# A two-layer encoder with a hierarchical mixture of experts: the first four experts as one block of four, two weight tiles outside the ring, fewer double buffers

## Chip, cores, metric

One core of a Trainium2 chip runs the whole program in one launch. The metric is the device time of a launch in microseconds (us); the time before is the median of three runs.

## What is computed

A sequence of 256 tokens of width 1024, in float32, goes through two layers. Each layer has an attention mixer (layer 0: differential and latent attention side by side; layer 1: dilated attention), a layer norm, a mixture of experts, and another layer norm. The mixture is where most bytes are: 32 experts per layer, each with a gate and an up matrix of 1024 x 512 and a down matrix of 512 x 1024. Every token is sent to two experts of one group:

```
coarse = xf @ w_group + b_group;  g_sel = argmax(coarse)
fine = (xf @ w_route + b_route)[group g_sel]
top_v, top_i = top_k(fine, 2)
gate = softmax(coarse)[g_sel] * softmax(top_v)
eid = g_sel * 8 + top_i
hb = silu(xb @ w_gate[e]) * (xb @ w_up[e]);  y = hb @ w_down[e]
out[token] += gate * y
```

The reference pads each expert to blocks of 256 rows; the result does not depend on that.

## The kernel before, in words

**Weights.** All large weights pass through `ring`, 18 buffers of 128 x 2048 float32 (one "piece" of 1,048,576 bytes each), issued on the queue of SP in program order. One expert is six pieces: two halves each of gate, up and down. A piece can be issued when the buffer that it takes, 18 allocations back, has been read for the last time. One more piece per layer, `lead`, has a tile of its own in the pool of the expert stage, outside the ring.

**Blocks.** The experts of a layer are worked off in blocks, listed in `BLOCKS` as (experts in the block, index of the first). A block fills the 128 stationary columns of TensorE: either two experts with 64 token slots each, or four experts with 32 slots each (`CAP`, `SMALL`). Experts 0 to 3 (`FIXED`) stand in the first two blocks, two experts with 64 slots each. The other 28 are sorted on the device by how many tokens they got (`ordered`); the four fullest (`HEAVY`) make two more blocks of two, and the other 24 make six blocks of four. Ten blocks in all. The numbers of the sorted experts, `ids`, are read by SP from a tile before it can issue their weights (`value_load`, L587); the weights of experts 0 to 3 need no such number, so they can be fetched while the router has not run.

**What one block does** (`expert_block`): the gate products `g` (L606), the up products `u` (L606), a small stage that makes `wcol` and `selT` for putting results back (`slot_side`), the nonlinearity and a transpose to `hT` (`hidden`), the down products `y` (L627), and `combine`, which adds the block's results to the residual `r` with matmuls `cb` (L563). The inputs of a block's experts are collected by matmuls with a 0/1 matrix `sel` into `xg` (`gather`, L532), for two blocks at a time. For the first pair only the 128 columns of block 0 are collected ahead; `fetch` collects the columns of block 1 in two parts inside block 0, one before `y` and one behind it.

**Fetching ahead.** Near the end of the mixer, `load_block` issues the 12 pieces of block 0; at the start of the expert stage it issues 6 pieces of block 1, and then `lead`, the last down piece of block 1 (`LATE`). Together with `lead` that is 19 pieces before the first product of the stage gives a buffer back. 5 more pieces of the 24 of experts 0 to 3 follow, and then the pieces of the sorted experts.

**Too many tokens.** When an expert has more tokens than its slots, `extra_block` runs behind the last block but one, once for each further 64 tokens (`lite` says by how much a slot count is below 64). It loads the whole expert again through POOL's queue, in pieces of 128 x 1024.

Of the kernel before, what the change touches and what calls it, by code (L numbers as in the profile page):

```python
# [28 lines left out]
SORTED = EXPERTS - FIXED  # L29
BLOCKS = [(2, i) for i in range(0, FIXED + HEAVY, 2)]  # L30
BLOCKS += [(4, i) for i in range(FIXED + HEAVY, EXPERTS, 4)]
MAX_EXTRA = (2 * T) // (SMALL + 1)
ALPHA = (2 * 2) ** 0.25
# [10 lines left out]
CLOCK = 43  # L44
LATE = 1, 11
WO_ORDER = (0, 4, 1, 5, 2, 6, 3, 7), tuple(range(8))
# [14 lines left out]
def trunk(ctx, tc, xT_d, x_d, wab_d, wla_d, wuq_d, wukv_d, woab_d, wc_d, wocd, wr_d, rb_d, gate_d, up_d, down_d,  # L61
# [324 lines left out]
    def route(pool, lg_ps, mvs, layer):  # L386
# [75 lines left out]
        def ordered(W):  # L462
# [22 lines left out]
            lite = t([32], "lite")  # L485
            v.memset(lite[:, 0:FIXED], 0.0)
            v.tensor_scalar(lite[:, FIXED:], place, float(HEAVY), float(CAP - SMALL), op0=OP.is_gt, op1=OP.mult)
# [21 lines left out]
    def slot_side(pool, sel, ws, ne, cap, name):  # L509
        n = ne * cap  # L510
        b = bank("slot" + name)
        for c in range(2):
            nc.tensor.matmul(b[0:n, 0:ne], lhsT=sel[:, c], rhs=ws[:, c], start=c == 0, stop=c == 1)
        for c in range(2):
            nc.tensor.transpose(b[0:n, 128 * (c + 1):128 * (c + 2)], sel[:, c], ident)  # L515
        wcol = pool.tile([128, 1], F32, tag="wcol", name="wcol" + name)
        for s in range(ne):
            nc.vector.tensor_copy(wcol[cap * s:cap * s + cap], b[cap * s:cap * s + cap, s:s + 1])  # L518
        selT = pool.tile([128, 256], F32R, tag="selT", name="selT" + name)
        nc.scalar.activation(selT[0:n], b[0:n, 128:384], AF.Copy)  # L520
        return wcol, selT, b

    def gather(xg, x, which, sel, o, n, name, evict=lambda kk: 1, first=False, todo=range(KK)):
        per = 512 // n
        for k0 in range(todo[0], todo[-1] + 1, 8 if first else per):
            bs = [bank("xg" + name) for _ in range(2 if first else 1)]
# [69 lines left out]

    def expert_block(pool, layer, p, ws, xg, side, r, fetch, rows):
        name = f"_{layer}_{p}"
        ne = BLOCKS[p][0]
        cap = 128 // ne  # L600
        o = 128 * (p % 2)
        gu = [bank("g" + name), bank("u" + name)]
# [19 lines left out]
        for k2 in range(2):  # L622
            for h in range(2):
                for k in (2 * k2, 2 * k2 + 1):
                    for s in range(ne):
                        w0 = k % 2 * 1024 + h * 512
                        nc.tensor.matmul(y_ps[h][cap * s:cap * s + cap], lhsT=hT[:, k, cap * s:cap * s + cap],  # L627
                                         rhs=ws[2, s, k // 2][:, w0:w0 + 512], start=k == 0, stop=k == 3)
        if p == 0:
            fetch(range(4, KK))  # L630
        return combine(pool, y_ps, side, 128, r, name, p == 0, accs), accs

    def extra_block(pool, layer, x, key, W, extra, lite, r):
# [10 lines left out]
        ohb = oh[:, None, :].to_broadcast([128, 2, 32])  # L644
        pr = pool.tile([128, 2, 2, 32], F32, tag="x_pr", name="x_pr")
# [4 lines left out]
        rem = pool.tile([128, 32], F32, tag="x_rem", name="x_rem")  # L650
        v.tensor_tensor(rem, extra, oh, op=OP.mult)
# [34 lines left out]
    def moe(layer, acc, x_in, xn, after):  # L686
        with tc.tile_pool(name=f"moe{layer}", bufs=2) as pool:
            lead = pool.tile([128, PIECE], F32, name=f"lead{layer}", bufs=1)
            xs = keep.tile([128, 2, D], F32, tag="xT", name=f"xs{layer}")
            ws = moe_w[layer]  # L690

            load_block(ws, layer, 0)
            load_block(ws, layer, 1, RING - 12)
            block, i = LATE
            e = BLOCKS[block][1] + i % 2
            nc.sync.dma_start(lead, down_d[layer][e, :, PIECE:2 * PIECE])
            ws[block][2, i % 2, 1] = lead
            lg_ps, mvs, last_lg, clk = mixer_norm(pool, acc, x_in, xn, layer)
# [4 lines left out]
            W = ids = None  # L703
            for q in range(len(BLOCKS) // 2):
                name = f"_{layer}_q{q}"
                ne, first = BLOCKS[2 * q]
                cap = 128 // ne
                if first < FIXED:
                    keys = key[:, :, first:first + 2 * ne]
                else:  # L710
                    keys = keyS[:, :, first - FIXED:first - FIXED + 2 * ne]
                sel = select(pool, keys, 2 * ne, cap, name, 1 if q == 0 else 2)
                xg = keep.tile([128, KK, 4 * CAP], F32, tag=("r", "gb")[q % 2], name="xg" + name)

                gather(xg, xs, 2 * layer, sel, 0, 2 * CAP if q == 0 else 4 * CAP, name,
                       (lambda kk: kk % 2 or kk > 3) if q == 0 else (lambda kk: kk // 2 % 2), q == 0)
# [88 lines left out]
    def heads_ab(pool, xT):  # L805
# [234 lines left out]
    def heads_c(pool, x, ws, res, gb):  # L1040
# [254 lines left out]
```

## Time and profile before

| | |
|---|---|
| time, median of 3 runs | 1176.53 us (1175.67 to 1176.67) |
| the profiled execution's own time | 1176.07 us |
| its span, first to last instruction | 1174.4 us |
| bytes moved | 445.80 MB, mean 380 GB/s over the span |
| TensorE busy | 1000.5 us (85%) |
| mean granted clock of TensorE | 0.956 |

The span is what the views below divide up; 1.67 us of the profiled execution lie outside it. "Busy" of TensorE (PE) counts matmuls whose ends are modelled, so 85% is not 85% of its peak. The views give the rate of all DMA engines in GB/s for any stretch of the span.

### The profile page before, as it was taken

How to read it: one execution, taken by the hardware profiler on the slowest of the kernel's cores; microseconds unless marked ns; L12 is line 12 of the kernel's file. 1: busy time of each engine (PE TensorE's matmuls, PEld its weight loads, DVE VectorE, ACT ScalarE, POOL GpSimd, SP SyncE). 2: the span in 40 equal slices, each digit the busy share in tenths (PEclk: the TensorE clock that was granted, in tenths of full speed). 3: DMA queues.
4: the chain of work that ended last, by engine and by line, in shares of the span. 5: the costliest groups of instructions: out<-in, count | busy, mean ns of one | idle time of the engine just before them, and what ended most of it. 6: DMA issues, size and time to landing. Idle time of an engine off the chain costs nothing. (4 is left out here: it accounts for less than half of the span.)

```text
span 1174.4 us, 14832 instructions
## 1 busy us (share of the span) xinstructions
PE 1000.5 (85%) x5568; PEld 478.2 (41%) x5568; DVE 374.5 (32%) x860; ACT 226.2 (19%) x495; POOL 50.8 (4%) x57
## 2 busy tenths in 40 slices
PE   8999999997787778778889999999977877697775
PEld 7787534342141213112578876343421311131222
DVE  5786822221020101010487768322210101010103
ACT  5565211010010001000445643110100100010001
POOL 0002000000000000000331120000000000000001
PEclk9999999999898989898999999999998989898897
DMA  9966798999999999999995566989999999999994
GB/s 362 424 235 241 286 427 352 427 422 427 427 427 427 426 425 427 427 425 427 426 412 180 156 235 254 427 351 426 424 427 426 426 428 427 425 426 426 425 427 187
DMA packets 65292, 445.80 MB, mean 380 GB/s; under 512 B 7680, under 2 KB 8448, under 8 KB 12992
## 3 DMA queue, kind: packets, MB, share of 16 engines
q1 hardware_dynamic: 62496, 436.15, 89.8%
q0 software_dynamic: 2432, 8.13, 2.0%
q8 instruction: 45, 0.74, 0.2%
q10 hardware_dynamic: 288, 0.52, 0.1%
q14 instruction: 31, 0.25, 0.1%
HBM read 443.73 MB, written 1.05 MB: 379 GB/s over the span
## 5 line engine op out<-in xcount | busy, mean ns | idle before, releaser
L606 PE MATMUL u<-w,xg_q 128*32 128x512 f32 (+1 forms) x1024 | 221.3, 705 | 57.8 <-DMA w<-in_up_dram 57.8
L627 PE MATMUL y<-w,hT 128*32 128x512 f32 (+1 forms) x1008 | 206.9, 602 | 36.4 <-DMA w<-in_down_dram 22.2
L606 PE MATMUL g<-w,xg_q 128*32 128x512 f32 (+1 forms) x1024 | 182.9, 627 | 43.7 <-DMA w<-in_gate_dram 36.3
L606 PEld LDWEIGHTS u<-w,xg_q 128*32 128x32 f32 (+1 forms) x1024 | 52.8, 132 | 210.2 <-DMA w<-in_up_dram 105.6
L627 PEld LDWEIGHTS y<-w,hT 128*32 128x32 f32 (+1 forms) x1008 | 55.6, 116 | 173.9 <-issue 92.6
L542 DVE TENSOR_TENSOR h<-h,u 128x512 f32<-128x512 f32 x20 | 13.8, 688 | 324.2 <-PE u L606 324.2
L606 PEld LDWEIGHTS g<-w,xg_q 128*32 128x32 f32 (+1 forms) x1024 | 46.4, 121 | 166.5 <-issue 91.6
L556 ACT ACTIVATE yh<-y,wcol 128x512 fp32r<-128x512 f32 x40 | 27.5, 687 | 395.0 <-PE y L627 395.0
L557 DVE SCALAR_TENSOR_TENSOR yl<-y,wcol,yh 128x512 fp32r<-128x512 f32 x40 | 29.9, 748 | 221.9 <-ACT yh L556 221.9
L532 PE MATMUL xg_q<-sel_q,xs 128*128 128x256 f32 (+1 forms) x384 | 74.3, 346 | 0.0
L532 PEld LDWEIGHTS xg_q<-sel_q,xs 128*128 128x128 f32 x384 | 63.6, 190 | 9.3 <-issue 1.9
L541 ACT ACTIVATE h<-g 128x512 f32<-128x512 f32 x20 | 11.9, 597 | 224.4 <-PE g L606 224.4
L518 DVE COPY wcol<-slot 32x1 f32<-32x1 f32 (+1 forms) x64 | 9.9, 155 | 140.6 <-PE slot L515 139.7
L572 DVE TENSOR_TENSOR x<-cb,x 128x512 f32<-128x512 f32 x64 | 40.7, 682 | 6.2 <-PE cb L563 5.9
L296 ACT ACTIVATE xg_q<-xg_q,pv 128x256 f32<-128x256 f32 (+1 forms) x60 | 26.9, 512 | 69.0 <-PE xg_q L532 66.0
L247 POOL DMA_DIRECT2D gb<-in_lnrow_dram x8 | 4.3, 542 | 665.7 <-PE u L606 653.8
L520 ACT ACTIVATE selT<-slot 128x256 fp32r<-128x256 f32 x20 | 7.7, 383 | 113.9 <-DVE wcol L518 113.9
L563 PE MATMUL cb<-yl,selT 128*128 128x512 f32 x72 | 26.5, 427 | 0.0
L563 PE MATMUL cb<-yh,selT 128*128 128x512 f32 x72 | 26.1, 421 | 0.0
L297 DVE TENSOR_SCALAR xg_q<-xg_q,pv 128x256 f32<-128x256 f32 (+1 forms) x36 | 17.5, 524 | 20.7 <-PE xg_q L532 19.8
L547 PE MATMUL hT<-con,h 128*128 128x128 f32 x80 | 13.1, 286 | 11.2 <-DVE h L542 10.7
L164 ACT ACTIVATE ec<-ec,stc 128x256 f32<-128x256 f32 x32 | 15.9, 498 | 16.6 <-DVE stc L162 16.6
(1060 smaller groups left out, 1277.9 us busy)
## 6 DMA issues: line engine op xcount, KB each, us to landing
w<-in_gate_dram SPq DMA_DIRECT2D x128, 1024.0 KB, 19.5
w<-in_up_dram SPq DMA_DIRECT2D x128, 1024.0 KB, 19.5
w<-in_down_dram SPq DMA_DIRECT2D x124, 1024.0 KB, 19.4
wqkc<-in_wc_dram SPq DMA_DIRECT2D x8, 1024.0 KB, 19.3
wqk<-in_wab_dram SPq DMA_DIRECT2D x4, 1024.0 KB, 13.3
wo<-in_woab_dram SPq DMA_DIRECT2D x4, 1024.0 KB, 11.3
gb<-in_lnrow_dram POOLq DMA_DIRECT2D x8, 512.0 KB, 8.3
wvc<-in_wc_dram SPq DMA_DIRECT2D x4, 1024.0 KB, 18.2
```

What stands on the lines that cost most here:

```text
L164: marks["exp"] = nc.scalar.activation(e[:, c], t[:, c], AF.Exp, bias=st[:, c:c + 1], scale=scale, accum_out=st[:, 2 + c:3 + c])
L296: return nc.scalar.activation(out, src, AF.Identity, bias=bb, scale=g)
L297: return nc.vector.tensor_scalar(out, src, g, bb, op0=OP.mult, op1=OP.add)
L532: nc.tensor.matmul(out[kk], lhsT=x[:, c, kk * 128:(kk + 1) * 128], rhs=sel[:, c, o:o + n], start=not first and c == 0, stop=c == 1 and (no ...
L542: nc.vector.tensor_tensor(h[0:n], h[0:n], u_ps[0:n], op=OP.mult)
L547: turn = nc.tensor.transpose(bv[:, k, 0:n], h[0:n, k * 128:(k + 1) * 128], ident[0:n, 0:n])
L556: last = nc.scalar.activation(yh[0:n, h], y_ps[h][0:n], AF.Copy, scale=wcol[0:n])
L557: nc.vector.scalar_tensor_tensor(yl[0:n, h], y_ps[h][0:n], wcol[0:n], yh[0:n, h].bitcast(F32), op0=OP.mult, op1=OP.subtract)
L563: last_mm = nc.tensor.matmul(b, lhsT=selT[0:n, c * 128:(c + 1) * 128], rhs=y[0:n, h], start=j == 0 and not accs, stop=j == 1)
L572: nc.vector.tensor_tensor(o, b, o, op=OP.add)
L606: up = nc.tensor.matmul(gu[j][cap * s:cap * s + cap], lhsT=xg[:, kk, o + cap * s:o + cap * s + cap], rhs=ws[j, s, kk // 4][:, kk % 4 * 512 ...
L627: nc.tensor.matmul(y_ps[h][cap * s:cap * s + cap], lhsT=hT[:, k, cap * s:cap * s + cap], rhs=ws[2, s, k // 2][:, w0:w0 + 512], start=k == ...
```

## The change

The first four experts become one block of four, with 32 slots each; nine blocks instead of ten, and `GROUPED` says which blocks share a `gather`: block 0 alone, then (1, 2), (3, 4), (5, 6), (7, 8). `fetch` is gone. Two tiles `leads` hold the second down halves of experts 2 and 3 (`LATE = 22, 23`), and `load_block` in the mixer issues 18 pieces (`RING`) of block 0. `lite` of experts 0 to 3 becomes 32. To make room, `selT`, `hT`, `x_oh` and `x_rem` have one buffer instead of two, and `x_pr` and `x_xg` share the buffers of `fo` and `hT`.

```diff
-BLOCKS = [(2, i) for i in range(0, FIXED + HEAVY, 2)]
+BLOCKS = [(4, 0)] + [(2, i) for i in range(FIXED, FIXED + HEAVY, 2)]
 BLOCKS += [(4, i) for i in range(FIXED + HEAVY, EXPERTS, 4)]
+GROUPED = [(0,)] + [(p, p + 1) for p in range(1, len(BLOCKS), 2)]
-LATE = 1, 11
+LATE = 22, 23
-            v.memset(lite[:, 0:FIXED], 0.0)
+            v.memset(lite[:, 0:FIXED], float(CAP - SMALL))
-        selT = pool.tile([128, 256], F32R, tag="selT", name="selT" + name)
+        selT = pool.tile([128, 256], F32R, tag="selT", name="selT" + name, bufs=1)
-        hT = pool.tile([128, 4, 128], F32, tag="hT", name="hT" + name)
+        hT = pool.tile([128, 4, 128], F32, tag="hT", name="hT" + name, bufs=1)
-            fetch(range(0, 4))
-        if p == 0:
-            fetch(range(4, KK))
-        xg = pool.tile([128, KK, CAP], F32, tag="x_xg", name="x_xg", bufs=1)
+        xg = pool.tile([128, KK, CAP], F32, tag="hT", name="x_xg", bufs=1)
-            lead = pool.tile([128, PIECE], F32, name=f"lead{layer}", bufs=1)
+            leads = [pool.tile([128, PIECE], F32, name=f"lead{layer}{i}", bufs=1) for i in range(2)]
+            for lead, i in zip(leads, LATE):
+                nc.sync.dma_start(lead, down_d[layer][i % 4, :, PIECE:2 * PIECE])
+                ws[0][2, i % 4, 1] = lead
             load_block(ws, layer, 0)
-            load_block(ws, layer, 1, RING - 12)
-            for q in range(len(BLOCKS) // 2):
+            for q, ps in enumerate(GROUPED):
-                ne, first = BLOCKS[2 * q]
-                cap = 128 // ne
+                ne, first = BLOCKS[ps[0]]
+                cap, n = 128 // ne, 128 * len(ps)
-                xg = keep.tile([128, KK, 4 * CAP], F32, tag=("r", "gb")[q % 2], name="xg" + name)
+                xg = keep.tile([128, KK, n], F32, tag=("r", "gb")[q % 2], name="xg" + name)
-        load_block(moe_w[0], 0, 0)
+        load_block(moe_w[0], 0, 0, RING)
```

On SP's queue in layer 0, at the start of the expert stage, before the change (a name `w_0_1_1_0` is layer, block, expert within the block, half; the tensor behind the arrow says whether it is gate, up or down):

```order
L76 DMA w_0_1_0_1_1223<-in_gate_dram 128x2048
L76 DMA w_0_1_1_1_1225<-in_gate_dram 128x2048
L696 DMA lead_1217<-in_down_dram 128x2048
L76 DMA w_0_1_0_0_1227<-in_up_dram 128x2048
L76 DMA w_0_1_1_0_1229<-in_up_dram 128x2048
L76 DMA w_0_1_0_1_1468<-in_up_dram 128x2048
L76 DMA w_0_1_1_1_1470<-in_up_dram 128x2048
L76 DMA w_0_1_0_0_1472<-in_down_dram 128x2048
L76 DMA w_0_1_1_0_1474<-in_down_dram 128x2048
L76 DMA w_0_1_0_1_1476<-in_down_dram 128x2048
L587 TENSOR_LOAD ids_1440
```

The same place of SP's queue in the changed kernel:

```order
L77 DMA w_0_0_2_1_1125<-in_up_dram 128x2048
L77 DMA w_0_0_3_1_1127<-in_up_dram 128x2048
L690 DMA lead_1229<-in_down_dram 128x2048
L690 DMA lead_1230<-in_down_dram 128x2048
L77 DMA w_0_0_0_0_1129<-in_down_dram 128x2048
L77 DMA w_0_0_1_0_1131<-in_down_dram 128x2048
L77 DMA w_0_0_2_0_1234<-in_down_dram 128x2048
L77 DMA w_0_0_3_0_1236<-in_down_dram 128x2048
L77 DMA w_0_0_0_1_1238<-in_down_dram 128x2048
L77 DMA w_0_0_1_1_1240<-in_down_dram 128x2048
L588 TENSOR_LOAD ids_1450
```

The read of `ids` stands behind the same number of pieces, 24. A second lead has come in front of the last two pieces that find a free ring buffer; of the pieces that wait for the stage's own products there are four, all down pieces of block 0, where there were five of block 1.

On TensorE in layer 0, from the end of block 0 before the change (`xg` with 128 columns is the second part of `fetch`, `g_1` the gate products of block 1, which are again two of experts 0 to 3):

```order
L627 MATMUL y_0_0_1550<-w_0_0_1_1_1119,hT_0_1525 64x512
L532 MATMUL xg_q_1567<-sel_q_1378,xs_1218 128x128 x8
L563 MATMUL cb_0_1586<-yh_0_1580,selT_0_1520 128x512
L563 MATMUL cb_0_1586<-yl_0_1581,selT_0_1520 128x512
L563 MATMUL cb_0_1590<-yh_0_1580,selT_0_1520 128x512
L563 MATMUL cb_0_1590<-yl_0_1581,selT_0_1520 128x512
L563 MATMUL cb_0_1594<-yh_0_1580,selT_0_1520 128x512
L563 MATMUL cb_0_1594<-yl_0_1581,selT_0_1520 128x512
L563 MATMUL cb_0_1598<-yh_0_1580,selT_0_1520 128x512
L563 MATMUL cb_0_1598<-yl_0_1581,selT_0_1520 128x512
L606 MATMUL g_1_1644<-w_0_1_0_0_1219,xg_q_1381 64x512
```

From the same place in the changed kernel, where `g_1` belongs to the two fullest of the sorted experts:

```order
L564 MATMUL cb_0_1656<-yh_0_1646,selT_0_1596 128x512
L564 MATMUL cb_0_1656<-yl_0_1647,selT_0_1596 128x512
L564 MATMUL cb_0_1660<-yh_0_1646,selT_0_1596 128x512
L564 MATMUL cb_0_1664<-yh_0_1646,selT_0_1596 128x512
L533 MATMUL xg_q_1714<-sel_q_1711,xs_1231 128x256 x2
L564 MATMUL cb_0_1660<-yl_0_1647,selT_0_1596 128x512
L564 MATMUL cb_0_1664<-yl_0_1647,selT_0_1596 128x512
L533 MATMUL xg_q_1714<-sel_q_1711,xs_1231 128x256 x2
L533 MATMUL xg_q_1721<-sel_q_1711,xs_1231 128x256 x4
L533 MATMUL xg_q_1728<-sel_q_1711,xs_1231 128x256 x4
L533 MATMUL xg_q_1735<-sel_q_1711,xs_1231 128x256 x4
L606 MATMUL g_1_1784<-w_0_1_0_0_1487,xg_q_1713 64x512
```

The gather with 256 columns for the two blocks of the fullest experts now stands directly behind block 0; before, a whole block of two experts stood between.

## Rows read from the trace of the kernel before

**Rows 1.** The page: span, and the rate in 40 equal slices.

```profile
span 1174.4 us, 14832 instructions
GB/s 362 424 235 241 286 427 352 427 422 427 427 427 427 426 425 427 427 425 427 426 412 180 156 235 254 427 351 426 424 427 426 426 428 427 425 426 426 425 427 187
```

**Rows 2.** The page: the queue of POOL, and issues by tile (KB, us to landing).

```profile
q0 software_dynamic: 2432, 8.13, 2.0%
...
w<-in_down_dram SPq DMA_DIRECT2D x124, 1024.0 KB, 19.4
...
gb<-in_lnrow_dram POOLq DMA_DIRECT2D x8, 512.0 KB, 8.3
```

**Rows 3.** The chain that ended last, in order of time: start, us, what.

```profile
1136.15 19.41 DMA w<-in_down_dram
...
1155.61 5.80 PE y L627 x28
```

**Rows 4.** Windows of both expert stages: us, busy of each engine, PEclk, DMA share, GB/s.

```profile
120.00:131.00 11.00, 10.99 (x72) 6.13 (x73) 9.83 (x35) 3.78 (x9) 0.00 (x0) 1.00 0.21 62
131.00:185.00 54.00, 51.77 (x261) 25.45 (x258) 25.96 (x44) 8.74 (x18) 0.00 (x0) 1.00 1.01 427
185.00:193.00 8.00, 8.00 (x38) 2.88 (x39) 0.16 (x1) 1.08 (x3) 0.00 (x0) 1.00 0.43 150
193.00:549.00 356.00, 285.24 (x1468) 93.86 (x1468) 47.92 (x94) 24.42 (x42) 1.05 (x2) 0.94 1.01 426
713.00:723.00 10.00, 9.99 (x63) 5.15 (x62) 8.99 (x30) 3.78 (x9) 0.00 (x0) 1.00 0.23 63
723.00:778.00 55.00, 52.77 (x266) 25.96 (x264) 26.03 (x43) 8.92 (x19) 0.00 (x0) 1.00 1.01 427
778.00:785.00 7.00, 7.00 (x34) 2.30 (x32) 0.00 (x0) 0.97 (x3) 0.00 (x0) 1.00 0.41 114
785.00:1155.00 370.00, 298.12 (x1560) 99.31 (x1556) 49.91 (x100) 24.73 (x43) 1.05 (x2) 0.94 1.01 426
```

**Rows 5.** The queue of SP in layer 0: issues in order of time.

```profile
106.09 0.33 SPq L696 DMA_DIRECT2D lead<-in_down_dram  x1
113.03 15.51 SPq L76 DMA_DIRECT2D w<-in_up_dram  x4
131.16 3.76 SPq L76 DMA_DIRECT2D w<-in_down_dram  x3
136.15 10.19 SPq L76 DMA_DIRECT2D w<-in_gate_dram  x4
```

**Rows 6.** Waits of SP's queue, 180 to 195 us: us in total, times, longest.

```profile
SPq L76 <- PE g L606: 14.4, 2, 12.0
```

**Rows 7.** TensorE in layer 0, in order of time: start, us, what.

```profile
124.05 7.09 PE L606 MATMUL g<-w,xg_q 128*64 128x512 f32 x32
...
142.33 7.09 PE L627 MATMUL y<-w,hT 128*64 128x512 f32 x32
149.35 2.05 PE L532 MATMUL xg_q<-sel_q,xs 128*128 128x128 f32 x16
...
178.33 1.02 PE L532 MATMUL xg_q<-sel_q,xs 128*128 128x256 f32 x4
...
185.78 7.09 PE L606 MATMUL g<-w,xg_q 128*64 128x512 f32 x32
...
244.95 7.07 PE L606 MATMUL g<-w,xg_q 128*32 128x512 f32 x64
```

**Rows 8.** VectorE (DVE) in layer 0, in order of time.

```profile
121.53 0.42 DVE L505 TENSOR_TENSOR sel_q<-con,key 128x256 f32<-128x256 f32 x1
...
122.47 0.29 DVE L449 TENSOR_TENSOR fo<-oh,lg 128x128 f32<-128x128 f32 x1
...
130.01 0.18 DVE L477 TENSOR_SCALAR ids<-idf 128x28 int32<-128x28 f32 x1
```

**Rows 9.** Windows with a lower granted clock, columns as in rows 4.

```profile
360.00:370.00 10.00, 7.09 (x28) 1.44 (x29) 0.00 (x0) 0.00 (x0) 0.00 (x0) 0.67 1.01 424
...
450.00:460.00 10.00, 10.00 (x47) 7.70 (x49) 5.80 (x10) 1.77 (x5) 0.00 (x0) 1.00 1.01 428
```

**Rows 10.** TensorE at the end of layer 0's last block.

```profile
565.99 2.76 PE L627 MATMUL y<-w,hT 128*32 128x512 f32 x18 [0.19 <-DMA w<-in_down_dram]
```

More of the change, by code (lines that the diff above doesn't have):

```diff
@@ L518, in slot_side, with gather @@
             nc.vector.tensor_copy(wcol[cap * s:cap * s + cap], b[cap * s:cap * s + cap, s:s + 1])
-        selT = pool.tile([128, 256], F32R, tag="selT", name="selT" + name)
+        selT = pool.tile([128, 256], F32R, tag="selT", name="selT" + name, bufs=1)
         nc.scalar.activation(selT[0:n], b[0:n, 128:384], AF.Copy)
         return wcol, selT, b
-    def gather(xg, x, which, sel, o, n, name, evict=lambda kk: 1, first=False, todo=range(KK)):
+    def gather(xg, x, which, sel, o, n, name, evict=lambda kk: 1, first=False):
         per = 512 // n
-        for k0 in range(todo[0], todo[-1] + 1, 8 if first else per):
+        for k0 in range(0, KK, 8 if first else per):
             bs = [bank("xg" + name) for _ in range(2 if first else 1)]
@@ L595, in load_block, with expert_block @@
                 w[j, e, o] = piece(src, name)
-    def expert_block(pool, layer, p, ws, xg, side, r, fetch, rows):
+    def expert_block(pool, layer, p, o, ws, xg, side, r, rows):
         name = f"_{layer}_{p}"
@@ L600, in expert_block @@
         cap = 128 // ne
-        o = 128 * (p % 2)
         gu = [bank("g" + name), bank("u" + name)]
@@ L635, in extra_block @@
         v = nc.vector
-        oh = pool.tile([128, 32], F32, tag="x_oh", name="x_oh")
+        oh = pool.tile([128, 32], F32, tag="x_oh", name="x_oh", bufs=1)
         v.tensor_scalar(oh, extra, 0.0, None, op0=OP.is_gt)
@@ L644, in extra_block @@
         ohb = oh[:, None, :].to_broadcast([128, 2, 32])
-        pr = pool.tile([128, 2, 2, 32], F32, tag="x_pr", name="x_pr")
+        pr = pool.tile([128, 2, 2, 32], F32, tag="rt_fo", name="x_pr", bufs=1)
         v.tensor_tensor(pr[:, 0], key, ohb, op=OP.mult)
@@ L649, in extra_block @@
         v.tensor_reduce(col, pr, axis=AX.X, op=OP.add)
-        rem = pool.tile([128, 32], F32, tag="x_rem", name="x_rem")
+        rem = pool.tile([128, 32], F32, tag="x_rem", name="x_rem", bufs=1)
         v.tensor_tensor(rem, extra, oh, op=OP.mult)
@@ L687, in moe @@
         with tc.tile_pool(name=f"moe{layer}", bufs=2) as pool:
-            lead = pool.tile([128, PIECE], F32, name=f"lead{layer}", bufs=1)
+            leads = [pool.tile([128, PIECE], F32, name=f"lead{layer}{i}", bufs=1) for i in range(2)]
             xs = keep.tile([128, 2, D], F32, tag="xT", name=f"xs{layer}")
             ws = moe_w[layer]
+            for lead, i in zip(leads, LATE):
+                nc.sync.dma_start(lead, down_d[layer][i % 4, :, PIECE:2 * PIECE])
+                ws[0][2, i % 4, 1] = lead
             load_block(ws, layer, 0)
-            load_block(ws, layer, 1, RING - 12)
[L694 to L697, printed above, removed]
             lg_ps, mvs, last_lg, clk = mixer_norm(pool, acc, x_in, xn, layer)
@@ L703, in moe @@
             W = ids = None
-            for q in range(len(BLOCKS) // 2):
+            for q, ps in enumerate(GROUPED):
                 name = f"_{layer}_q{q}"
-                ne, first = BLOCKS[2 * q]
-                cap = 128 // ne
+                ne, first = BLOCKS[ps[0]]
+                cap, n = 128 // ne, 128 * len(ps)
                 if first < FIXED:
-                    keys = key[:, :, first:first + 2 * ne]
+                    keys = key[:, :, first:first + len(ps) * ne]
                 else:
-                    keys = keyS[:, :, first - FIXED:first - FIXED + 2 * ne]
-                sel = select(pool, keys, 2 * ne, cap, name, 1 if q == 0 else 2)
-                xg = keep.tile([128, KK, 4 * CAP], F32, tag=("r", "gb")[q % 2], name="xg" + name)
-                gather(xg, xs, 2 * layer, sel, 0, 2 * CAP if q == 0 else 4 * CAP, name,
+                    keys = keyS[:, :, first - FIXED:first - FIXED + len(ps) * ne]
+                sel = select(pool, keys, len(ps) * ne, cap, name, 1 if q == 0 else 2)
+                xg = keep.tile([128, KK, n], F32, tag=("r", "gb")[q % 2], name="xg" + name)
+                gather(xg, xs, 2 * layer, sel, 0, n, name,
                        (lambda kk: kk % 2 or kk > 3) if q == 0 else (lambda kk: kk // 2 % 2), q == 0)
@@ L721, in moe @@
                         ids, (keyS, WS), extra, lite, n_i = ordered(W)
-                def fetch(todo):
-                    gather(xg, xs, 2 * layer, sel, 2 * CAP, 2 * CAP, name, todo=todo)
-                for p in (2 * q, 2 * q + 1):
+                for p in ps:
                     if p + 1 < len(BLOCKS):
                         load_block(ws, layer, p + 1, AHEAD if p == LOOP_AFTER else 99, ids)
-                    o = 128 * (p % 2)
+                    o = 128 * (p - ps[0])
                     at = BLOCKS[p][1]
@@ L734, in side @@
                         return slot_side(pool, sel[:, :, o:o + 128], w, ne, cap, f"_{layer}_{p}")
-                    last, accs = expert_block(pool, layer, p, ws.pop(p), xg, side, r, fetch, lambda: affine_from(r, xs, gb))
+                    last, accs = expert_block(pool, layer, p, o, ws.pop(p), xg, side, r, lambda: affine_from(r, xs, gb))
                     if p == LOOP_AFTER:
@@ L1128, in heads_c @@
         attend(6)
-        load_block(moe_w[1], 1, 0)
+        load_block(moe_w[1], 1, 0, RING)
         ws = op.prep_piece(3)
```

## The prediction

> **What bounds the kernel now.** I first read the rate by slices [rows 1]. Outside three stretches it stands at 422 to 428 GB/s: the weights come as fast as this core ever fetches, and a piece of 1,048,576 bytes takes 2.456 us at 427 GB/s. The chain of waits ends the same way: down pieces landing, then the products on the last one [rows 3]. So the time is that of the bytes plus the time in which the queue has nothing to move. No bytes are added or removed, so what a change is worth is how much of that dead time it removes.
>
> The two mixers are one part of it (slices with 156 to 286 GB/s); there TensorE and VectorE work and the ring has no free buffer. The windows of the expert stages [rows 4] show the rest. In layer 0 the rate is 62 GB/s from 120 to 131 us: of these 11 us, 62 / 427 x 11 = 1.6 us were used, 9.4 us were dead. The rate then holds 427 until 185, falls to 150 over 8 us (8 - 150 / 427 x 8 = 5.2 us dead), and holds 426 until the stage ends. Layer 1 repeats it: 63 GB/s over 10 us (8.5 us dead), and 114 GB/s over 7 us (7 - 114 / 427 x 7 = 5.1 us dead).
>
> The first hole is the wait for the router: 19 pieces are in, and no buffer is free until the gate products, from 124.05 us [rows 7], have used up a half. The second hole is also a full ring, 50 us into the stage. SP's queue waited 12.0 us at a stretch for gate products there [rows 6]. Count it: blocks 0 and 1 hold 24 pieces, one of them in `lead`, so they give 23 buffers back; counting full rate from 131 - 1.6 = 129.4 us, 23 pieces last 23 x 2.456 = 56.5 us, to 185.9. TensorE is late: two blocks of two experts and the 256-column gather take from 124.05 to 185.78, and only then do gate products free the next buffers [rows 7]. TensorE is busy 51.8 of 54 us in that stretch, at a granted clock of 1.00 [rows 4], so here it sets the pace.
>
> **The change, part by part.**
>
> *One block in place of two.* A block of four with 32 columns each has its 64 gate records in 7.07 us, a block of two with 64 columns its 32 in 7.09 us [rows 7]: a block costs the same whether it uses up 24 pieces or 12. Experts 0 to 3 therefore cost one block and not two. Block 0 keeps its gate, up and transpose times; the two parts of `fetch` (2.05 us each at most [rows 7]) go, so `y`, which ran from 142.33 to 149.4, runs from about 141 to 148, and the gather for the next two blocks starts near 150 rather than at 178.33. From the start of this gather through two blocks of two and the next gather to the first block of four, TensorE takes 244.95 - 178.33 = 66.6 us [rows 7]; in the changed kernel that block starts near 216.6, and its first half frees buffers near 220. When does the ring run dry now? After the first products, block 0 gives back 22 ring buffers (24 less two leads), all by 148.5, and the two blocks of two give 24. 46 pieces last 113 us from 129.4, to 242. In between the tightest point is the first 22, used up at 183.4, while block 1's gate products free more from about 161. The margins are 22 us each. So the second hole closes in both layers: 5.2 + 5.1 = **10.3 us**. What is late next is the data: TensorE reaches the first sorted block of four near 217 us, its eighth gate piece is the 36th and arrives at 129.4 + 88.4 = 217.8, and from there on the kernel waits for pieces as now.
>
> *One more tile outside the ring.* The order on SP's queue is the second lead, then the two up-to-now last free buffers. The first lead went out at 106.09, and up pieces were issued from 113.03 [rows 5]; the second lead has no user before it and goes behind the first. One piece more is in before the hole, which is 9.4 and 8.5 us deep, so all of its 2.456 us falls into dead time, even if it goes out only with the up pieces at 113.03: the three pieces then need 7.4 us and have 16.4 until 129.4. Two layers: **4.9 us**; the bounds are 0, if it came only after the hole, and 4.9.
>
> The rate on which this rests is 427 GB/s, held over 54 us [rows 4]. The Trainium skill, DMA: Bandwidth & Descriptors, Where 436 GB/s comes from, says that between HBM and SBUF the HBM side binds near 358 GB/s per core, beside a measurement of 425 on the same page. By 358 a piece would last 2.93 us (an estimate), this term would be 5.9 and the sum 16.7; the trace disagrees, so that is no case here.
>
> *A narrower `sel` ahead of block 0.* The two comparisons that make it have 128 columns, not 256. One with 256 took 0.42 us, an operation with 128 columns 0.29 [rows 8]. Both stand on VectorE's path to the gather: 2 x 0.13 = 0.26 us earlier per layer, **0.5 us** in all. The bounds are 0 and 0.84 (nothing left of them, both layers, would be 1.7).
>
> *Edits that I cost at nothing.* The read of `ids` comes behind 24 pieces as before, but four of them now go out at once when the first gate halves are used up, so SP gets there near 129.5 instead of 135; `ids` was made at 130.01 and the first sorted gate piece went out 1.2 us behind the last issue before it (131.16 + 3.76 to 136.15) [rows 5, 8]. By then four pieces, 9.8 us of data, are under way, so it hides until `ids` is 8 us later. Behind this read stand all sorted pieces. Block 0's last four down pieces are now fetched inside the block: issued by 129, landed by 129.4 + 9.8 = 139.2, needed from 141 (the halves of the second step from 145). If they landed only at the usual 19.4 us behind their issue [rows 2], `y` would start some 7 us late; the 22 us of margin in the ring hide that, and the whole price without that cover would be 7 us a layer. One buffer instead of two for `selT` and `hT`: the next use is a whole gate and up stage, 14 us, behind the last reader, and TensorE works in order, so 0. One more 512-column comparison for a later `sel` stands ahead of the copy of `hT` on VectorE: up to 0.7 us of TensorE's time, inside the same margin. The issues on SP and POOL are as many as before.
>
> **Sum.** 10.3 + 4.9 + 0.5 = 15.7 us. The profiled execution of 1176.07 us becomes 1160.4 (span 1158.7). The median of the runs shown is 0.46 us above the profiled execution, so I forecast a median of **1160.8 us**. What each layer saves moves everything behind it, because the rate is full to the end of both stages [rows 4]. A difference under 0.2%, 2.4 us, cannot be told from none.
>
> Around the sum lies the granted clock at the two ends, where nothing hides it: the last 28 `y` records of layer 1 took 5.80 us [rows 3], 0.207 each, the last 18 of layer 0 took 2.76, 0.153 each [rows 10]. Layer 1's end could be 1.5 us shorter, layer 0's 1 us longer; other phases of the same waits could cost some 3 us. The likeliest case's own range is 1157 to 1164.
>
> **Rivals.**
>
> *The clock falls in the blocks of two (slower).* Where TensorE waits for pieces the granted clock drops: 0.67 in one window of 10 us with 2.9 us idle [rows 9], 0.94 over the whole stretch [rows 4], against 1.00 without waits. The blocks of two now come when data are short, so their first products could run at 1.2 instead of 2.4 GHz. At a mean clock c the 66.6 us become 66.6 / c; buffers are late once 150 + 66.6 / c + 3.5 passes 242, at c = 0.75, the gain of a layer is gone at 0.69, and at 0.5 a layer loses 133 + 153.5 - 242 = 45 us less 7.9, so 1176.5 + 2 x 37 = 1250 us. Against it: a TensorE that falls behind has no waits, and without waits it ran at 1.00 [rows 4, 9]. 2 in 100. [...]
>
> *Extra rounds (slower).* Experts 0 to 3 now have 32 slots. One with more tokens costs a round of `extra_block` per layer: twelve half pieces of 524,288 bytes, at least 14.7 us at 427 GB/s, at most 12 x 8.3 / 2 = 50 us by POOL's issue to landing with two buffers [rows 2]. One round would leave about 1175.5, one in each layer 1190. It decides from 33 tokens on. The traffic of POOL's queue before, 8.13 MB [rows 2], is its row loads and strips alone (8 x 0.524 + 20 x 0.197), so no round ran. Working the router out on the reference's inputs gives experts 0 to 3 at most 17 tokens in layer 0 and 22 in layer 1. 1 in 100.
>
> *Only the lead counts.* If the second hole reappears a block later, 4.9 + 0.5 is left: 1171.1 us. The margin of 22 us speaks against it. 6 in 100.
>
> *Only the hole counts, or a third of it is given back.* If the second lead is late, or block 0's down pieces start the stage late, some 5 us are lost: 1166. 12 in 100.
>
> *It does nothing*, as the mixer of layer 1 or the end takes the gain up: 1176.5. The mixer starts from the last expert piece, so I see no place for it. 2 in 100.
>
> **How the numbers follow.** The forecast has the remaining 77 in 100. The range reaches from the low end of its own range, 1157, to the case of 1166: 1156.5 to 1167. Faster: 77 + 6 + 12 = 95 in 100; same 2; slower 2 + 1 = 3.
>
> **What would show it.** Right: a full rate from about 130 us to the end of layer 0's experts with no dip near 186, and the same near 779 less 8 us; a dead time of some 7 us, not 9.4, at the start; SP's queue with no wait of 12 us for gate products; gate products of block 1 from about 157. Wrong: a hole in the rate between 150 and 245 us, waits of `y` of block 0 on down pieces that last over 7 us, a mean clock under 0.75 from 150 to 217, or traffic on POOL's queue above 8.13 MB.

## The result, and the profile after

The changed kernel takes 1160.96 us (median of 4 runs, 1158.91 to 1161.67), the kernel before 1176.6 us (4 runs beside it, 1175.67 to 1178.03). The ratio is 0.9863, with a 95% interval of 0.9846 to 0.988: faster by 1.4%. Forecast were 1160.8 us. The profiled execution took 1160.28 us, so its span fell from 1174.4 to 1158.6 us, by 15.8.

The page of the changed kernel, the lines that answer to [rows 1] and [rows 2]:

```profile
span 1158.6 us, 14602 instructions
...
GB/s 361 424 242 257 273 427 427 427 427 426 428 425 428 427 425 427 427 425 428 424 421 189 154 232 280 427 427 425 428 426 427 426 427 426 427 427 427 425 426 190
...
q0 software_dynamic: 2432, 8.13, 2.0%
```

The slices with 352 and 351 GB/s, one in each layer, are gone; behind the first hole the rate stays at 424 to 428 to the end of an expert stage. POOL's queue carried 8.13 MB as before, so no extra round ran. The windows of both expert stages of the changed kernel, columns as in [rows 4] (layer 1 by 8 us earlier; the row of 131 to 185 us is the stretch of full rate that ran into the second hole before):

```profile
120.00:131.00 11.00, 11.00 (x106) 6.50 (x107) 9.37 (x36) 3.79 (x9) 0.00 (x0) 0.98 0.19 50
131.00:185.00 54.00, 51.54 (x318) 22.81 (x308) 26.52 (x48) 6.76 (x12) 0.00 (x0) 1.00 1.01 424
185.00:193.00 8.00, 8.00 (x40) 2.84 (x36) 0.84 (x2) 0.60 (x1) 0.00 (x0) 1.00 1.01 425
193.00:541.00 348.00, 272.17 (x1339) 86.54 (x1342) 42.21 (x84) 21.55 (x37) 1.05 (x2) 0.94 1.01 427
705.00:715.00 10.00, 10.00 (x94) 5.08 (x97) 8.87 (x31) 3.79 (x9) 0.00 (x0) 1.00 0.20 60
715.00:770.00 55.00, 52.55 (x316) 23.27 (x310) 26.35 (x46) 6.76 (x12) 0.00 (x0) 1.00 1.01 426
770.00:777.00 7.00, 7.00 (x36) 2.56 (x34) 0.93 (x3) 0.98 (x2) 0.00 (x0) 1.00 1.01 426
```

The second hole is closed in both layers: 425 GB/s where [rows 4] have 150, and 426 where they have 114. The first hole looks unchanged in these windows, 50 and 60 GB/s, though a piece more was fetched: that is taken up below.

TensorE of the changed kernel in layer 0, in order of time, answering to [rows 7] (`clk` are filler products that keep the clock up while the router runs):

```profile
116.98 3.35 PE L104 MATMUL clk<-ones_b 128*128 128x128 bf16 x30
120.12 0.23 PE L432 MATMUL rk<-M,tri_b 128*128 128x32 bf16 x1
...
125.26 7.07 PE L606 MATMUL g<-w,xg_q 128*32 128x512 f32 x64
...
142.56 4.06 PE L626 MATMUL y<-w,hT 128*32 128x512 f32 x34 [1.36 <-DVE hT L549]
...
151.06 1.03 PE L533 MATMUL xg_q<-sel_q,xs 128*128 128x256 f32 x4
...
152.40 6.21 PE L533 MATMUL xg_q<-sel_q,xs 128*128 128x256 f32 x28
158.53 7.09 PE L606 MATMUL g<-w,xg_q 128*64 128x512 f32 x32
...
218.68 7.07 PE L606 MATMUL g<-w,xg_q 128*32 128x512 f32 x64
...
228.56 1.04 PE L606 MATMUL u<-w,xg_q 128*32 128x512 f32 x2 [0.17 <-DMA w<-in_up_dram]
```

Block 0 with four experts has its 64 gate records in 7.07 us, as a block of two had its 32 in 7.09; `y` waits for `hT` and not for down pieces; the first sorted block of four starts at 218.68 us, where it started at 244.95, and the first wait for a piece comes 10 us behind it. SP's queue of the changed kernel at the start of the stage, and its waits from 112 to 262 us (us in total, times, longest), answering to [rows 5] and [rows 6]:

```profile
106.07 0.82 SPq L690 DMA_DIRECT2D lead<-in_down_dram  x2
113.00 18.48 SPq L77 DMA_DIRECT2D w<-in_down_dram  x6
132.72 2.71 SPq L77 DMA_DIRECT2D w<-in_gate_dram  x4
```

```profile
SPq L77 <- DMA w<-in_down_dram: 32.9, 19, 3.0
...
SPq L77 <- PE g L606: 15.4, 2, 15.1
```

The one long wait for gate products, 15.1 us, is the first hole (issues 2 and 3 of the six down pieces lie on either side of it); the second one of 12.0 us is gone. Most of SP's other waits are now put down to its own transfers; the longest for a down piece is 3.0 us.

### The profile page after: what moved, and what is told of

Read it like the earlier page. It is cut to its first block, busy times and chain, and to the rows that moved or that the text cites. A ratio compares the mean times of both kernels' runs of the same rounds, so it can differ in the third digit from the quotient of the medians.

```text
span 1158.6 us, 14602 instructions
## 1 busy us (share of the span) xinstructions
PE 970.4 (84%) x5468; PEld 457.6 (39%) x5468; DVE 362.7 (31%) x844; ACT 215.6 (19%) x471; POOL 50.9 (4%) x57
## 3 DMA queue, kind: packets, MB, share of 16 engines
q0 software_dynamic: 2432, 8.13, 2.0%
HBM read 443.73 MB, written 1.05 MB: 384 GB/s over the span
## 4 chain that ended last, share of the span: by engine, by line
DMA 58%; PE 33%; DVE 6%; ACT 2%; issue 1%; SPq 0%; ACTq 0%; DVEq 0%
DMA w<-in_down_dram 22%; DMA w<-in_gate_dram 17%; DMA w<-in_up_dram 17%; PE y L626 4%; PE g L606 4%; PE xg_q L533 3%; PE u L606 3%; DMA wqkc<-in_wc_dram 1%; PE qkc L189 1%; PE qkc L190 1%; PE qkc L191 1%; PE mix L190 1%; PE mix L189 1%; PE mix L191 1%; PE cb L564 1%
## 5 line engine op out<-in xcount | busy, mean ns | idle before, releaser
L606 PE MATMUL u<-w,xg_q 128*32 128x512 f32 (+1 forms) x1024 | 208.8, 681 | 68.8 <-DMA w<-in_up_dram 68.8
L606 PE MATMUL g<-w,xg_q 128*32 128x512 f32 (+1 forms) x1024 | 175.6, 663 | 40.3 <-DMA w<-in_gate_dram 36.2
L606 PEld LDWEIGHTS u<-w,xg_q 128*32 128x32 f32 (+1 forms) x1024 | 48.4, 125 | 212.9 <-DMA w<-in_up_dram 123.2
L606 PEld LDWEIGHTS g<-w,xg_q 128*32 128x32 f32 (+1 forms) x1024 | 42.5, 122 | 161.9 <-issue 85.9
L533 PE MATMUL xg_q<-sel_q,xs 128*128 128x256 f32 (+1 forms) x320 | 66.2, 360 | 0.0
L533 PEld LDWEIGHTS xg_q<-sel_q,xs 128*128 128x128 f32 x320 | 56.2, 190 | 7.5
L542 ACT ACTIVATE h<-g 128x512 f32<-128x512 f32 x18 | 10.8, 598 | 213.7 <-PE g L606 213.7
L573 DVE TENSOR_TENSOR x<-cb,x 128x512 f32<-128x512 f32 x56 | 34.6, 680 | 0.0
L297 ACT ACTIVATE xg_q<-xg_q,pv 128x256 f32<-128x256 f32 (+1 forms) x44 | 20.9, 534 | 61.5 <-PE xg_q L533 58.5
L564 PE MATMUL cb<-yh,selT 128*128 128x512 f32 x64 | 22.1, 421 | 0.0
L548 PE MATMUL hT<-con,h 128*128 128x128 f32 x72 | 11.8, 287 | 10.8 <-DVE h L543 10.6
L104 PEld LDWEIGHTS <-ones_b 128*128 128x128 bf16 x252 | 17.8, 111 | 3.8 <-issue 2.3
```

Of the source, the lines that this page charges most:

```text
L104: nc.tensor.matmul(b[:, 0:128], lhsT=ones_b, rhs=ones_b, start=True, stop=True)
L297: return nc.scalar.activation(out, src, AF.Identity, bias=bb, scale=g)
L533: nc.tensor.matmul(out[kk], lhsT=x[:, c, kk * 128:(kk + 1) * 128], rhs=sel[:, c, o:o + n], start=not first and c == 0, stop=c == 1 and (no ...
L564: last_mm = nc.tensor.matmul(b, lhsT=selT[0:n, c * 128:(c + 1) * 128], rhs=y[0:n, h], start=j == 0 and not accs, stop=j == 1)
L573: nc.vector.tensor_tensor(o, b, o, op=OP.add)
L606: up = nc.tensor.matmul(gu[j][cap * s:cap * s + cap], lhsT=xg[:, kk, o + cap * s:o + cap * s + cap], rhs=ws[j, s, kk // 4][:, kk % 4 * 512 ...
```

## The experiments

**What each theory says.** Theory A: the time is the bytes at 427 GB/s plus the dead time of the queue, and dead time is a count of pieces against the moment when buffers come back. A piece that is fetched outside the ring fills dead time in front of the stage, but that is only kept if the ring does not run full again further on. Theory B: the parts of the sum are independent, 10.3 us for the block and 4.9 for the tile, each to be had alone.

Two windows show it in all kernels. From 95 to 140 us (45 us around the start of layer 0's expert stage) a piece more is 1.0486 MB / 45 us = 23 GB/s. From 180 to 193 us (13 us around the second hole) a piece is 81 GB/s. For the kernel before:

```profile
95.00:140.00 45.00, 43.95 (x279) 29.96 (x276) 34.52 (x96) 16.13 (x35) 2.05 (x3) 1.00 0.70 264
...
180.00:193.00 13.00, 13.00 (x62) 7.29 (x62) 2.80 (x6) 2.09 (x5) 0.00 (x0) 1.00 0.66 258
```

For the changed kernel:

```profile
95.00:140.00 45.00, 44.98 (x338) 30.77 (x337) 33.35 (x94) 15.77 (x34) 2.04 (x3) 0.96 0.72 275
...
180.00:193.00 13.00, 12.95 (x60) 5.11 (x56) 3.89 (x6) 1.97 (x3) 0.00 (x0) 1.00 1.01 425
```

**e1: the kernel before with the second tile.** The double buffers are cut as in the change, and the room holds a second `lead`; the blocks stay.

```diff
-LATE = 1, 11
+LATE = 10, 11
...
-        selT = pool.tile([128, 256], F32R, tag="selT", name="selT" + name)
+        selT = pool.tile([128, 256], F32R, tag="selT", name="selT" + name, bufs=1)
...
-            lead = pool.tile([128, PIECE], F32, name=f"lead{layer}", bufs=1)
+            leads = [pool.tile([128, PIECE], F32, name=f"lead{layer}{i}", bufs=1) for i in range(2)]
...
+            for lead, i in zip(leads, LATE):
+                nc.sync.dma_start(lead, down_d[layer][BLOCKS[1][1] + i % 2, :, PIECE:2 * PIECE])
+                ws[1][2, i % 2, 1] = lead
```

> The kernel before, with a second tile outside the ring (the last two down pieces of block 1) and the single buffers of the change, but with two blocks of two for experts 0 to 3. Theory A (the fetch is bound by buffers given back): by the second hole 18 ring buffers plus 24 pieces used up have been fetched, whatever stands outside the ring, since each tile outside takes a piece that would have given a ring buffer back. So the first hole gets 2.4 us shorter per layer, the second 2.4 us longer, and the time stays at 1176.6 us (1174.5 to 1178.5). Theory B (the parts add): each layer saves 2.456 us, 1171.7 us.

Measured: 1177.91 us (12 runs, 1175.89 to 1181.66) against 1177.09 of the kernel before; ratio 1.0011 (0.9998 to 1.0023). The same two windows of e1:

```profile
95.00:140.00 45.00, 43.95 (x278) 29.98 (x276) 34.42 (x95) 16.14 (x35) 1.95 (x3) 1.00 0.74 287
...
180.00:193.00 13.00, 13.00 (x61) 7.21 (x61) 2.70 (x6) 2.19 (x5) 0.00 (x0) 1.00 0.49 180
```

The piece is there, 287 against 264 GB/s, and it is missing again from 180 to 193 us, 180 against 258. Theory B falls: the tile alone is worth nothing.

**e2: the change with one tile.**

```diff
-LATE = 22, 23
+LATE = (23,)
...
-            leads = [pool.tile([128, PIECE], F32, name=f"lead{layer}{i}", bufs=1) for i in range(2)]
+            leads = [pool.tile([128, PIECE], F32, name=f"lead{layer}{i}", bufs=1) for i in range(len(LATE))]
```

> The changed kernel with one tile outside the ring instead of two. Theories A and B: the second hole stays closed, the first is 2.456 us longer per layer than in the changed kernel, so 1161.0 + 4.9 = 1165.9 us (1163.5 to 1168). Rival (the second tile is hidden anyway): 1161.

Measured: 1165.26 us (5 runs, 1162.94 to 1167.86); ratio 0.99 (0.9881 to 0.992). With the hole closed the second tile is worth 1165.26 - 1160.96 = 4.3 us, and the block of four alone 1177.09 - 1165.26 = 11.8 us. The windows have 264 GB/s, as before with one tile, and 424:

```profile
95.00:140.00 45.00, 44.70 (x347) 30.07 (x345) 34.77 (x100) 15.89 (x35) 2.23 (x3) 1.00 0.71 264
...
180.00:193.00 13.00, 12.95 (x58) 5.06 (x56) 4.12 (x8) 1.97 (x3) 0.00 (x0) 1.00 1.01 424
```

**e3: one tile, and the double buffers back.** As e2, with `selT` and `hT` in two buffers again and `x_xg` in a tile of its own.

```diff
...
-        hT = pool.tile([128, 4, 128], F32, tag="hT", name="hT" + name, bufs=1)
+        hT = pool.tile([128, 4, 128], F32, tag="hT", name="hT" + name)
...
```

> The kernel of the run with one lead, but with two buffers again for selT and hT, and a tile of its own for x_xg. Theory A: single buffers cost nothing, since the next use is a whole gate and up stage behind the last reader: equal to the run with one lead, 1165.9 us within 2 us. Rival (the single buffers cost a wait in each of nine blocks, some 0.2 us or more): 2 to 4 us less, 1162 to 1164.

Measured: 1166.7 us (6 runs, 1163.57 to 1168.43); ratio 0.9907 (0.9888 to 0.9926). The interval overlaps that of e2: the single buffers of `selT` and `hT` cost nothing that can be told. Those of `x_oh` and `x_rem` are used by `extra_block` alone, of which no round ran; no run here tests them.

**e4: a third tile.** A further down piece goes ahead of the stage in two halves. One stands in the unused half of the tile in which the first `xg` is gathered (`front`), one in a new tile of 1024 columns (`half`), for which `h` takes the buffers of `y1` and `sel` of `extra_block` those of `fo`. Two things more differ from the changed kernel: `sel` has one buffer in place of two, and `mixer_norm` stands ahead of `load_block` in the program.

```diff
+HALVED = 21
...
+            front = keep.tile([128, PIECE], F32, tag="r", name=f"front{layer}")
+            halves = [front[:, PIECE // 2:], pool.tile([128, PIECE // 2], F32, name=f"half{layer}", bufs=1)]
+            for j, half in enumerate(halves):
+                o = PIECE + j * PIECE // 2
+                nc.sync.dma_start(half, down_d[layer][HALVED % 4, :, o:o + PIECE // 2])
+            ws[0][2, HALVED % 4, 1] = halves
```

> The changed kernel with a third piece outside the ring: one half in the unused half of the tile of the first xg, one in room won by putting h in the tile of yl. Theory A: the first hole is still some 7 us deep, so another 2.456 us per layer go: 1161.0 - 4.9 = 1156.1 us (1153.5 to 1158.5). Rival (the first hole is used up, or h now waits for the sorting on VectorE and TensorE starts the stage later): 1161 or more.

Measured: 1154.82 us (5 runs, 1153.95 to 1157.94); ratio to the kernel before 0.9817 (0.9798 to 0.9836). It beats both kernels, the changed one by 6.1 us. The window has one piece more again:

```profile
95.00:140.00 45.00, 44.16 (x343) 29.56 (x340) 33.80 (x97) 15.74 (x35) 1.72 (x3) 1.00 0.82 315
```

**e5 and e6: how much room is there behind block 0?** The prediction puts the margin at 22 us. Filler products (128x128, bf16) on TensorE between block 0 and the gather of blocks 1 and 2 use it up, 270 of them in e5 and 540 in e6.

```diff
+                if q == 1:
+                    with tc.issue_after(last.ins):
+                        keep_clock(bank("pad" + name), 270)
```

> The changed kernel with 270 more filler products of 128x128 on TensorE in each layer, between block 0 (the first block of four) and the gather of block 1, about 15 us by the price of the fillers in its trace (30 or so in 1.84 us). Nothing else moves. Theory A (only the hand-back of the ring's buffers counts, and block 1 has some 22 us to spare): the buffers of block 1 then come back at about 176 us, ahead of the 184 us at which the ring would run dry, so there is no hole and the time is 1161 us, +-2. Rival (TensorE's work ahead of block 1 is on the path): two layers of 15 us, 1191 us.

> As e5_pad_15us with 540 fillers, about 30 us in each layer. Theory A: the buffers of block 1 come back at about 191 us, 7 us after the ring has run dry, and with the 2 us that the queues take to start again the transfers stand still for some 9 us in each layer, from about 184 us on: 1179 us (1174 to 1184). Rival 1 (no buffer is ever missing at block 1, so the second hole of before had another cause): 1161 us. Rival 2 (TensorE's work is on the path in full): 1221 us.

Measured: e5 1160.04 us (4 runs, 1159.18 to 1160.46), ratio 0.9848 (0.9831 to 0.9864); e6 1180.76 us (10 runs, 1178.33 to 1182.23), ratio 1.0025 (1.0016 to 1.0035). Fifteen us more on TensorE in each layer cost nothing; thirty cost 1180.76 - 1160.96 = 19.8 us in two layers. TensorE (the gate products of block 1) and the windows of e5, which has no second hole:

```profile
172.20 7.09 PE L606 MATMUL g<-w,xg_q 128*64 128x512 f32 x32
```

```profile
95.00:140.00 45.00, 44.34 (x344) 29.72 (x342) 34.79 (x98) 16.12 (x35) 1.89 (x3) 1.00 0.75 290
...
180.00:193.00 13.00, 12.14 (x62) 4.54 (x60) 1.69 (x4) 0.38 (x1) 0.00 (x0) 1.00 1.01 425
```

The same of e6, where the second hole has come back:

```profile
187.31 7.09 PE L606 MATMUL g<-w,xg_q 128*64 128x512 f32 x32
```

```profile
180.00:193.00 13.00, 13.00 (x68) 8.18 (x67) 1.99 (x4) 2.04 (x4) 0.00 (x0) 1.00 0.36 130
```

From e5 to e6 the gate products of block 1 move by 15.1 us, so the fillers of e6 are some 30.2 us. The hole is (1 - 130 / 427) x 13 = 9.0 us. Layer 1 has the same, (1 - 252 / 427) x 22 = 9.0 us, and layer 0 has a further one of (1 - 326 / 427) x 8 = 1.9 us when the first sorted block of four begins:

```profile
230.49 8.78 PE L626 MATMUL y<-w,hT 128*64 128x512 f32 x32 [1.17 <-DVE hT L549]
```

```profile
248.00:256.00 8.00, 8.00 (x72) 2.23 (x70) 0.00 (x0) 1.62 (x3) 0.00 (x0) 1.00 0.87 326
...
778.00:800.00 22.00, 21.54 (x103) 10.68 (x101) 3.35 (x8) 3.02 (x6) 0.00 (x0) 1.00 0.62 252
```

Together they are 19.9 us, and 19.8 were lost. The first room is therefore about 30.2 - 9.0 = 21 us, where 22 were forecast; the small hole fits the second margin of the count, also used up. Part of that one is TensorE's clock: the `y` products of the second block of two took 8.78 us where the others take 7.1, at a granted clock of 0.72 from 230 to 236 us.

**e7: no tile at all.** `LATE = ()`, with the block of four.

> The changed kernel with no tile outside the ring at all (the last four down pieces go through the ring as the others do). Theory A (with the block of four only the first hole is left, and each tile outside the ring takes the transfer time of one piece, 2.45 us, from it in each layer): 4.9 us above the kernel with one such tile, 1170 us (1168.5 to 1172). Rival (the first tile of before is worth nothing by itself, as the second one was before the block of four): 1165 us.

Measured: 1170.64 us (4 runs, 1169.01 to 1172.75); ratio 0.9945 (0.9928 to 0.9961). The first tile is worth 1170.64 - 1165.26 = 5.4 us, as the theory of the count has it. The windows have one piece less than e2 in front, and no second hole:

```profile
95.00:140.00 45.00, 44.50 (x345) 29.88 (x343) 34.80 (x99) 16.12 (x35) 2.03 (x3) 1.00 0.65 242
...
180.00:193.00 13.00, 12.95 (x58) 4.99 (x56) 3.89 (x6) 1.38 (x2) 0.00 (x0) 1.00 1.01 425
```

**e8: the kernel before without its tile.**

```diff
-            lead = pool.tile([128, PIECE], F32, name=f"lead{layer}", bufs=1)
...
-            block, i = LATE
-            e = BLOCKS[block][1] + i % 2
-            nc.sync.dma_start(lead, down_d[layer][e, :, PIECE:2 * PIECE])
-            ws[block][2, i % 2, 1] = lead
```

> The kernel before without its one tile outside the ring (that down piece goes through the ring as the others do). Theory A (with blocks of two the transfers stand still twice, and by the second time what counts is how many pieces fit before block 1's buffers come back, so a piece taken out of the first wait is paid back in the second, as e1_before_second_lead showed for one tile more): one tile less lengthens the first stop by some 2.4 us and shortens the second by as much, no change, 1177.5 us (1175.5 to 1179.5). Rival (a tile outside the ring is worth its transfer time in any kernel, and the null of e1 came from its single buffers): 4.9 us slower, 1182.5 us.

Measured: 1176.83 us (10 runs, 1175.35 to 1182.6) against 1177.92; ratio 0.9998 (0.9981 to 1.0015). No change. A piece less in front, and a piece more in the second window (344 against 258 GB/s), so the second hole gives back what the first one takes:

```profile
95.00:140.00 45.00, 44.01 (x279) 30.05 (x277) 34.64 (x97) 16.15 (x35) 2.17 (x3) 1.00 0.65 237
...
180.00:193.00 13.00, 13.00 (x62) 7.41 (x62) 2.92 (x6) 2.04 (x4) 0.00 (x0) 1.00 0.89 344
```

All kernels side by side (median us; GB/s of the two windows):

| tiles outside the ring | blocks of two first: us | 95:140 | 180:193 | block of four first: us | 95:140 | 180:193 |
|---|---|---|---|---|---|---|
| 0 | 1176.83 (e8) | 237 | 344 | 1170.64 (e7) | 242 | 425 |
| 1 | 1177.09 (before) | 264 | 258 | 1165.26 (e2) | 264 | 424 |
| 2 | 1177.91 (e1) | 287 | 180 | 1160.96 (the change) | 275 | 425 |
| 3 | not run | | | 1154.82 (e4) | 315 | 425 |

On the left each tile brings a piece into the first window and takes it out of the second; on the right nothing is taken back, and a tile is worth (1170.64 - 1154.82) / 3 = 5.3 us, near the 4.9 of two transfers at full rate. The kernels were timed in four sets, in which the kernel before had 1176.6 to 1177.92 us; by the ratios to it a tile is worth (0.9945 - 0.9817) x 1177 / 3 = 5.0 us. The 275 of the change is the one figure out of step; e5, the same up to 148 us, has 290 (last section).

## Why the prediction was right, point by point

**The second hole: right.** 10.3 us were forecast for closing it, 10.8 with the narrower `sel`. At one tile outside the ring the block alone gave 11.8 us, and the windows have the full rate in both layers. That the cause is the moment when the buffers of block 1 come back, and not TensorE's work as such, e5 and e6 show: 15 us more work are free, 30 bring the hole back at the forecast place, with a room of 21 us where the count had 22. What TensorE did came at the forecast times, if the 1.5 us of the last section are taken off: `y` of block 0 at 142.56 to about 149.6 (forecast 141 to 148), the next gather near 151 (150), the gate products of block 1 at 158.53 (157), the first sorted block of four at 218.68 (216.6).

**The second tile: right in size, wrong in where it shows, and priced as if it stood alone.** 4.9 us were forecast, 4.3 came (e2 to the change; the intervals of the two ratios leave some 3 us either way, and the three tiles of the table together give the size better). But the text expected a dead time of 7 us in place of 9.4 in the windows at the stage's start, and they show (1 - 50 / 427) x 11 = 9.7 us. Of these, 1.5 us are the slow fillers of this profile (last section); e5, which has none in layer 0, shows (1 - 89 / 427) x 11 = 8.7 us:

```profile
120.00:131.00 11.00, 11.00 (x106) 5.64 (x108) 9.84 (x35) 3.94 (x10) 0.00 (x0) 1.00 0.28 89
```

Most of the piece moved in an earlier gap: the issue of the first lead and the issue of the up pieces lie 7 us apart [rows 5], and one transfer of 2.5 us did not fill that. In layer 0, the kernel before, then the changed kernel:

```profile
110.00:116.00 6.00, 6.00 (x46) 5.36 (x44) 4.53 (x13) 3.86 (x10) 0.00 (x0) 1.00 0.81 287
```

```profile
110.00:116.00 6.00, 6.00 (x46) 5.37 (x44) 4.54 (x13) 3.88 (x10) 0.00 (x0) 1.00 1.04 419
```

132 GB/s over 6 us are 0.8 of the piece's 1.05 MB. In layer 1 the whole piece is seen in the 86 us around the router; the kernel before, then the changed kernel:

```profile
644.98:730.98 86.00, 85.86 (x584) 64.17 (x583) 65.97 (x189) 41.05 (x98) 10.51 (x12) 1.00 0.60 207
```

```profile
637.53:723.53 86.00, 85.81 (x649) 63.72 (x648) 66.27 (x189) 41.06 (x98) 10.50 (x12) 1.00 0.62 220
```

13 GB/s over 86 us are 1.1 MB, one piece. It was dead time all the same, since these gaps and the hole behind them are one stretch in which more could be fetched than was.

**The rival that only the tile counts had a wrong price.** It put 1171.1 us on a second hole that comes back. e1 shows that with a second hole there the tile gives nothing, so that case would have been about 1176. It didn't come, so the forecast isn't touched, but the terms of the sum were not independent as the text took them to be: the 4.9 us depend on the 10.3.

**The clock in the blocks of two: it did not fall in the changed kernel.** The rows of 131 to 193 us and of 715 to 777 us have a granted clock of 1.00, the full 2.4 GHz; so has the stretch from 193 to 218 us, in which the second block of two ends. That it can fall there, e6 shows with its 0.72. Over the rest of the stage, where TensorE waits for pieces, the mean is 0.94, as before. The Trainium skill, TensorE: Matmul & The Clock Gate, HAM oscillation — how this bites in real kernels, describes a kernel in which the wait for data behind each group of matmuls is longer than the group's own work, and every group starts at the half clock. The changed kernel is not that case, and no run here shows it: TensorE is busy for 272 of the 348 us, and its longest wait for a piece there is 1.8 us.

**Edits costed at nothing: right where tried.** `y` waited for `hT` and for no down piece; SP read `ids` without a gap, the sorted gate pieces following the last down piece 1.2 us behind (131.48 to 132.72); the single buffers of `selT` and `hT` cost nothing that e3 could tell. From the router product of layer 1 to the first gate product pass 10.72 us (697.53 to 708.25) where 10.99 passed (704.98 to 715.97): 0.27 less by the narrower `sel`, forecast 0.26.

**Where the 15.8 us of the profiled pair lie.** Layer 0 gives 6.45: its last block's results (`fin`) begin at 563.31 us where they began at 569.76. Forecast were (10.3 + 4.9 + 0.5) / 2 = 7.85; 1.47 are lost again at the start of the stage (last section), so 6.4 were to be expected. Layer 1's mixer gives 1.0 that the sum doesn't have: its router product comes 7.45 us earlier. In the first 30 us of this mixer the granted clock was 0.94 before and 1.00 now. The products `vc` behind a wait of 1.8 us mostly took 0.63 us each before and 0.40 now, and over these few the lead grew from 6.44 us (592.33 to 585.89) to 7.92 (595.85 to 587.93), of which some 0.5 went again before the router. The kernel before, then the changed one:

```profile
570.00:600.00 30.00, 25.86 (x177) 20.41 (x177) 24.39 (x37) 14.83 (x33) 17.40 (x12) 0.94 1.01 426
...
592.92 0.63 PE L190 MATMUL vc<-vc0h13wh,xl 128*128 128x512 f32 x1
```

```profile
563.55:593.55 30.00, 25.24 (x180) 19.75 (x179) 25.06 (x40) 15.86 (x36) 17.46 (x12) 1.00 1.01 424
...
586.23 0.40 PE L191 MATMUL vc<-vc0h13wh,xl 128*128 128x512 f32 x1
...
697.53 1.87 PE L362 MATMUL lg<-wr,rT 128*128 128x36 f32 x16
```

Layer 1's experts give 7.8, where 7.85 were forecast: the last 28 `y` records, which wait for a down piece with 1.4 us of idle time in both, begin at 1140.34 us and not at 1155.61, so 15.27 - 7.45. They then take 5.26 us and not 5.80, since the last 18 have the full clock; 0.5 more. In the changed kernel:

```profile
1140.34 1.04 PE L626 MATMUL y<-w,hT 128*32 128x512 f32 x2 [1.40 <-DMA w<-in_down_dram]
1141.60 1.06 PE L626 MATMUL y<-w,hT 128*32 128x512 f32 x8 [0.22 <-DMA w<-in_down_dram]
1142.84 2.76 PE L626 MATMUL y<-w,hT 128*32 128x512 f32 x18 [0.17 <-DMA w<-in_down_dram]
```

6.45 + 1.0 + 7.8 + 0.5 = 15.8. In this pair 1.5 us lost to the clock in one place and 1.5 won by it in two others offset one another; that the forecast is met to a tenth is luck, that it is met within 2 us isn't.

## What to carry to other kernels

When transfers pace a kernel through a ring of buffers, find every stretch in which the queue stands still, and count pieces between them: a buffer added ahead of one stop is worth its transfer time only if no later stop of the same ring gives it back. So close the last stop first, and add buffers after. To test a margin, pad the engine that is said to have it, once within it and once beyond; two runs tell the size and show whether the mechanism is the one named.

## What the hardware showed that was not expected

The filler products under the router don't always keep the clock. A finer window of the changed kernel in layer 0:

```profile
118.00:120.00 2.00, 2.00 (x21) 2.00 (x20) 0.72 (x6) 0.30 (x1) 0.00 (x0) 0.50 0.99 418
```

TensorE had no pause there, and yet the granted clock was 0.50, half of 2.4 GHz. The 30 fillers took 3.35 us (116.98 above), where they took 1.84 in the same place of the kernel before and of all other kernels run here. The rank product `rk`, which stands behind them on TensorE, came late (120.12 where it came at 118.68), and with it everything up to the first gate products, which stand at 125.26 and not at 123.8. That is 1.5 us more of the first hole, and the 275 GB/s of the table: a piece of transfer time is 23 GB/s there, so the 15 GB/s that are missing against e5's 290 are 1.6 us. The same was seen in layer 1, with 2.98 us in e1, 3.00 in e3, 3.34 in e6 and 3.39 in e8. So it comes and goes with no regard to the change, in 5 of the 20 places (two layers in ten profiles). What decides it stays open; a filler ahead of a short product that others wait for costs its whole slow length when it falls there.
